# The SwiGLU's last 1024 hidden features: 768 of them by seven products, and a third weight sum made by an adding DMA

## The chip, the cores and the metric

The kernel runs on one core of a Trainium2 chip. The metric is the time of one execution on the device in microseconds (us), lower is better. A core has five engines with queues of their own: PE (matrix products), DVE (vector), ACT (activation), POOL (a second, slower vector engine) and SP (which here only issues DMAs). They meet through semaphores.

## What is computed

One inference step of a hybrid layer over 576 tokens (512 of a prompt, 64 of a sample), 1024 features wide: half a SwiGLU, a mixer, half a SwiGLU, a last norm.

```python
def swiglu(x, w_in, w_out):                  # w_in 1024 x 8192, w_out 4096 x 1024
    a, b = jnp.split(x @ w_in, 2, axis=-1)
    return (jax.nn.silu(a) * b) @ w_out
# layer: x + 1/2 swiglu(norm(x)); + mixer(norm(.)); + 1/2 swiglu(norm(.)); then norm
# mixer: one projection w_in (1024 x 9752), three branches, three projections, gates, w_out
```

All is float32. The transposed activations lie as (128 features) x (8 blocks) x (576 tokens).

## The kernel before

**Products in three parts.** A float32 operand is split into a rounded high part and the rest (`split`: a copy on ACT, L288, a subtraction on DVE, L289). A product is high x high + high x low + low x high, so each 128 x 128 weight block meets each token tile in three matmuls. `ph` and `pl` are the two parts of 512 columns of weights; they live in rings of six.

**Units of seven products.** Most of the work is done in units in the manner of Strassen and Winograd. A unit is two output blocks of 128 features, a reduction over 8 blocks (2 x 4), and two halves of 288 tokens; eight block products become seven. The products are called X1, X2, X3, X4, A11, A22, A21. Each multiplies a weight operand (a block of 128 x 512, or a sum of such blocks) with an activation operand (`T`, for the layer's input, or `T2`, for the hidden features of the SwiGLU). Each is 12 matmuls of 288 columns: 4 blocks x 3 parts (`product`, L616). Results add up in banks of the accumulator: X1, X3, A22, X2 in one, X4 and A21 in a second, A11 in a third, and between two products to one bank ACT or DVE must have read it.

**Weight sums.** For unit n, SP loads two blocks (`fetch_sums`, L460, 512 KB) into `wx`; POOL issues an adding DMA of another 512 KB onto them (L461): X1's operand and X2's. SP loads single blocks into `wr` (L467). In the SwiGLU X3's and X4's operands are made by POOL, in place on X1's tile: add block 2, and later block 3 (L472). In the mixer they go to tiles of their own (`wy`). `stream` works through the units: the operands of a product are made five products ahead (`AHEAD`), and products of two neighbouring units are interleaved by a written-out `order`, where (1, t) is the product t of the unit before:

```python
order = ((0, self.T_X1), (1, self.T_A22), (0, self.T_A11), (1, self.T_A21), (0, self.T_X3), (1, self.T_X2),
         (0, self.T_X4))
```

A planner then sets the order of instructions on every engine, by its own costs and the priorities that the program gives (`high_priority` for reading banks and for the norms).

**A SwiGLU** (`ffn`). The 4096 hidden features are four groups c of 1024, eight units j each. The first four of group 0 are computed plainly (`gemm`, L260), while the operands `T` are made; the rest are units of the stream. When two hidden blocks are ready, `hidden_operands` makes their share of `T2` (five differences on DVE, seven splits), in steps put between products (`tick`). Four units `out(c, m)` then multiply group c with w_out and add to the residual (`residual`, L655); they run between units 1 and 2 of group c + 1. Group 3 is different: its hidden blocks are only split (`hidden_parts`) into YH, YL, which take the place of T2's tiles, and after the stream a plain tail multiplies them with w_out: two passes (i = 6, 7) of 512 rows, eight outputs, two halves of 256 and 320 tokens (`HALVES`). The second pass does most outputs half by half (`half_major`), so that the norm behind it can begin on a finished half while the other is multiplied.

**What follows.** After the first SwiGLU the norm makes XH, XL (`scaled`, L338 and L339), squares (L296, L299, L300) and `rs`, the factor of each token; six plain projections in `branches`, the operands `T` of the mixer (`operands`, L434 to L446), and then the mixer's stream (`pairs`) with 35 units, while the branches' own work runs as jobs between products. After the second SwiGLU `norm_out` squares and scales the output (L299, L396), multiplies the upper half by `rs` (L422) and transposes the lower one (L408 to L415).

The functions that the change touches:

Of the kernel before, what the change touches and what calls it, by code (L numbers as in the profile page):

```python
# [35 lines left out]
NB = 63  # L36
NS = 115
FH = 288
NPLAIN = 4
BUFS = {"g": 9, "t": 5, "P": 4, "Q": 2, "bias": 2}  # L40
# [1 line left out]
FBUFS = {"P": 5, "g": 5, "s": 3}  # L42
# [39 lines left out]
class Hybrid:  # L82
# [112 lines left out]
    def squares(self, tag):  # L195

        pool, bufs = self.sqp
        if pool is self.op:
            return self.op.tile([128, T], F32, name=bufs[tag], tag=bufs[tag], bufs=2)[:, :320]
        return pool.tile([128, 320], F32, name=tag, tag=tag, bufs=bufs[tag])  # L200

    def sm(self):
# [40 lines left out]
        return pool.tile(list(shape), dt, name=tag, tag=tag, bufs=WBUFS[tag])  # L243

    def parts(self, src):
        return self.split(src, self.ring("ph", F32R), self.ring("pl", F32R))

    def col(self, name, n0):

# [202 lines left out]
    def fetch_sums(self, desc):  # L452


        nc = self.nc
        i = len(self.splan)
        self.splan.append(desc)
        src = self.I["sblk"][i].rearrange("p (q c) -> p q c", q=4)
        x12 = self.ring("wx", shape=(128, 2, 512))
        nc.sync.dma_start(x12, src[:, 0:2, :])  # L460
        return {"x12": x12, "src": src}, lambda: nc.gpsimd.dma_start(x12, src[:, 1:3, :], accum_op=ALU.add)  # L461

    def fetch(self, raw):

        for q in (2, 3, 0) if self.mixer else (0, 2, 3):
            raw[q] = self.ring("wr")
            self.nc.sync.dma_start(raw[q], raw["src"][:, q, :])  # L467

    def operand(self, raw, t):

        x12 = raw["x12"]
        add = lambda o, one, two: self.nc.gpsimd.tensor_tensor(o, one, two, op=ALU.add)  # L472
        if not self.mixer:

            if t in (self.T_X3, self.T_X4):
                add(x12[:, 0, :], x12[:, 0, :], raw[2 if t == self.T_X3 else 3])
            x3 = x4 = x12[:, 0, :]
        else:
            if t in (self.T_X3, self.T_X4) and "x3" not in raw:
                raw["x3"], raw["x4"] = self.ring("wy"), self.ring("wy")  # L480
                add(raw["x3"], x12[:, 0, :], raw[2])
                add(raw["x4"], raw["x3"], raw[3])
            x3, x4 = raw.get("x3"), raw.get("x4")
        return self.parts({self.T_X1: x12[:, 0, :], self.T_X2: x12[:, 1, :], self.T_X3: x3, self.T_X4: x4,
                           self.T_A11: raw[0], self.T_A22: raw[2], self.T_A21: raw[3]}[t])

    def stream(self, seq, order, banks):

# [31 lines left out]
    def pairs(self, seq):  # L520

        nc = self.nc
        order = ((0, self.T_X1), (0, self.T_A11), (1, self.T_A22), (0, self.T_X4), (0, self.T_X3), (1, self.T_X2),
                 (0, self.T_A21))
        H = (slice(0, FH), slice(FH, T))

        def tmp(ps, scale):  # L530
            o = self.gp.tile([128, FH], F32, name="uv", tag="uv", bufs=4)
            with self.tc.high_priority(offset=EVAC):
                nc.scalar.activation(o, ps, AF.Copy, scale=scale)  # L533
            return o

        def emit(ps, scale, other=None, op=None):
            def go(dst, a=0, b=FH, func=None):
                with self.tc.high_priority(offset=EVAC):
                    if other is None:
                        nc.scalar.activation(dst, ps[:, a:b], func or AF.Copy, scale=scale)  # L540
                        return
                    nc.vector.scalar_tensor_tensor(dst, ps[:, a:b], scale, other[:, a:b], op0=ALU.mult, op1=op)
                if func:
                    nc.scalar.activation(dst, dst, func)
            return go

        def pair(tiles, done):
            ((name, c1), s1, put1), ((_, c2), s2, put2) = tiles
            o = {}

            def on(t, ps):
                if t == self.T_X1:
                    o["v"] = tmp(ps, s1)
                elif t == self.T_X4:
                    o["m6"] = tmp(ps, s2)
                elif t == self.T_A11:
                    put1(1, H[1], emit(ps, s1, o["v"], ALU.add))
                elif t == self.T_X3:
                    o["u"] = tmp(ps, s2)
                elif t == self.T_A21:  # L560
                    put2(1, H[1], emit(ps, s2, o["u"], ALU.subtract))
                elif t == self.T_A22:
                    put2(0, H[0], emit(ps, -s2, o["m6"], ALU.add))
                else:
                    put1(0, H[0], emit(ps, s1))
                    if done:
                        done()
            return (name, 0, c1, c2), self.T, on
# [40 lines left out]
    def product(self, ps, ops, moving, start):  # L609
        self.tick()  # L610
        hi, lo = ops
        th, tl = moving
        for kk in range(4):
            wsl = slice(kk * 128, (kk + 1) * 128)
            for i, (wt, xx) in enumerate(((hi, th), (hi, tl), (lo, th))):
                self.nc.tensor.matmul(ps, wt[:, wsl], xx[:, kk, :], start=(start and kk == 0 and i == 0),  # L616
                                      stop=(kk == 3 and i == 2), skip_group_check=True)

    def swiglu(self, done):

# [56 lines left out]
            put(one, t)  # L677
            yield 1

    def hidden_parts(self, slot, g):  # L680
        self.split(g.rearrange("p h t -> p (h t)"), self.YH[:, slot, :], self.YL[:, slot, :])
        yield 1

    def ffn(self, x, g0, win, wout, name, last=(0, 1)):

        nc = self.nc
# [21 lines left out]
        def evac_o(ot):  # L710
            def go(h, ps, sl):
                nc.vector.scalar_tensor_tensor(x[:, ot, sl], ps, 0.5, x[:, ot, sl], op0=ALU.mult, op1=ALU.add)
            return go


        def at(c, j):
            return (8 * c + (j if c == 3 else j % 2 * 4 + j // 2)) * 128

        boxes = [{} for _ in range(NPLAIN)]
        tiles = []  # L720
# [17 lines left out]
        got, free = {}, [True]  # L738

        def flush():  # L740

            if not free[0]:
                return
            for c, j in sorted(got):
                if c == 3:
                    self.jobs.append(self.hidden_parts(j, got.pop((c, j))))
                elif j % 2 == 0 and (c, j + 1) in got:
                    self.jobs.append(self.hidden_operands(j // 2, got.pop((c, j)), got.pop((c, j + 1))))
                    if j == 6:
                        free[0] = False  # L750

        def unit(c, j):
            def done(g):
                got[c, j] = g
                flush()
            return (win, 0, 4096 + at(c, j), at(c, j)), self.T, self.swiglu(done)

        def out(c, m):
            def done():
                free[0] = True  # L760
                if c == 2:
                    self.hidden_tiles(name)
                flush()
            return (wout, 1024 * c, 256 * m, 256 * m + 128), self.T2, self.residual(x, m, done if m == 3 else None)

        for j, box in enumerate(boxes):
            got[0, j] = box["g"]
# [765 lines left out]
def pack(plans, inp):  # L1533
    plan, splan = plans
    a = {k: np.asarray(v) for k, v in inp.items()}
    f32 = np.float32
# [15 lines left out]
    sb = np.empty((NS, 128, 4, 4, 128), f32)  # L1552
    for i, (n, r0, c1, c2) in enumerate(splan):
        for q, (c, r) in enumerate(((c1, r0), (c1, r0 + 512), (c2, r0 + 512), (c2, r0))):
            sb[i, :, q] = w[n][r:r + 512, c:c + 128].reshape(4, 128, 128).transpose(1, 0, 2)
# [53 lines left out]
```

## Time and profile before

| | |
|---|---|
| median of three runs | 1939.52 us (1937.3 to 1940.52) |
| the profiled execution | 1944.79 us, its span 1943.1 us |
| granted clock of PE in it | 0.991 |
| units of seven products | 40 + 35 + 40 = 115 |
| the first SwiGLU's stream, by its products | 65.8 to about 532 us |
| the mixer's stream | 626.1 to about 1203 us |
| the second SwiGLU's stream | 1425 to about 1881 us |

Rows of the profile name the source line of the kernel before (L616), the engine, the tiles written and read (out<-in, buffer numbers left out), a count, and then busy time, mean duration of one in ns, and the idle time of the engine just before, with what ended it. PE is a matmul, PEld the load of its weights. Matmuls are pipelined: one takes 0.3 us by its record, while the next starts 0.12 to 0.15 us after it. A stretch's row has the busy us and the number of instructions of PE, PEld, DVE, ACT and POOL, the granted clock, the share of the DMA engines, and GB/s. A row of waits has the total, the number and the longest.

### The profile page before, as it was taken

How to read it: one execution, taken by the hardware profiler on the slowest of the kernel's cores; microseconds unless marked ns; L12 is line 12 of the kernel's file. 1: busy time of each engine (PE TensorE's matmuls, PEld its weight loads, DVE VectorE, ACT ScalarE, POOL GpSimd, SP SyncE). 2: the span in 40 equal slices, each digit the busy share in tenths (PEclk: the TensorE clock that was granted, in tenths of full speed). 3: DMA queues.
4: the chain of work that ended last, by engine and by line, in shares of the span. 5: the costliest groups of instructions: out<-in, count | busy, mean ns of one | idle time of the engine just before them, and what ended most of it. 6: DMA issues, size and time to landing. Idle time of an engine off the chain costs nothing. (4 is left out here: it accounts for less than half of the span.)

```text
span 1943.1 us, 37678 instructions
## 1 busy us (share of the span) xinstructions
PE 1887.2 (97%) x13901; PEld 1823.6 (94%) x13901; DVE 1524.6 (78%) x2715; ACT 1089.5 (56%) x2486; POOL 680.1 (35%) x656
## 2 busy tenths in 40 slices
PE   9999999999999999999999998999999999999998
PEld 8899999999999878888888888999999999999998
DVE  8998998988768767667777775745898888988865
ACT  4554654655544777767675765324555455554544
POOL 5343333333202234323435353440233334334311
PEclk9999999999999999899999999999999999999999
DMA  7267666666742545753667557742236666666631
GB/s 241 74 160 173 159 163 163 159 172 163 185 131 80 156 117 159 200 147 108 183 165 183 155 152 213 241 143 88 77 99 165 163 157 172 166 157 167 159 94 60
DMA packets 129440, 294.69 MB, mean 152 GB/s; under 512 B 14289, under 2 KB 26193, under 8 KB 129257
## 3 DMA queue, kind: packets, MB, share of 16 engines
q1 hardware_dynamic: 100072, 205.67, 32.7%
q0 software_dynamic: 19696, 72.10, 20.5%
q10 hardware_dynamic: 9488, 14.53, 2.6%
q8 instruction: 109, 1.79, 0.4%
q14 instruction: 75, 0.61, 0.1%
HBM read 272.87 MB, written 19.38 MB: 150 GB/s over the span
## 5 line engine op out<-in xcount | busy, mean ns | idle before, releaser
L616 PE MATMUL acc<-TH,ph 128*128 128x288 f32 x3220 | 968.0, 301 | 27.4 <-ACT uv L533 11.8
L616 PE MATMUL acc<-TL,ph 128*128 128x288 f32 x3220 | 955.4, 297 | 0.6 <-DVE TL L289 0.6
L616 PE MATMUL acc<-TH,pl 128*128 128x288 f32 x3220 | 955.0, 298 | 1.0 <-DVE pl L289 0.9
L616 PEld LDWEIGHTS acc<-TH,ph 128*128 128x128 f32 x3220 | 607.5, 189 | 46.9 <-ACT uv L533 15.5
L616 PEld LDWEIGHTS acc<-TL,ph 128*128 128x128 f32 x3220 | 609.4, 189 | 4.9 <-issue 3.7
L616 PEld LDWEIGHTS acc<-TH,pl 128*128 128x128 f32 x3220 | 608.4, 189 | 4.8 <-DVE pl L289 2.2
L289 DVE TENSOR_TENSOR pl<-wr,ph 128x512 fp32r<-128x512 f32 x471 | 429.4, 919 | 76.9 <-ACT ph L288 64.5
L288 ACT CAST ph<-wr 128x512 fp32r<-128x512 f32 x471 | 287.9, 620 | 267.9 <-PE acc L616 141.3
L289 DVE TENSOR_TENSOR pl<-wx,ph 128x512 fp32r<-128x512 f32 x390 | 328.1, 845 | 44.5 <-ACT ph L288 37.9
L288 ACT CAST ph<-wx 128x512 fp32r<-128x512 f32 x390 | 237.4, 621 | 201.3 <-POOL wx L472 110.2
L472 POOL TENSOR_TENSOR wx<-wx,wr 128x512 f32<-128x512 f32 x160 | 246.3, 1539 | 188.2 <-DVE pl L289 150.4
L461 POOL DMA_DIRECT2D wx<-in_sblk x115 | 101.6, 901 | 524.1 <-DMA wx<-in_sblk 154.7
L260 PE MATMUL acc<-YH,ph 128*128 128x256 f32 (+1 forms) x768 | 226.5, 298 | 6.3 <-ACT YH L288 5.8
L260 PE MATMUL acc<-YL,ph 128*128 128x320 f32 (+1 forms) x768 | 227.1, 297 | 2.3 <-DVE YL L339 1.9
L260 PE MATMUL acc<-YH,pl 128*128 128x256 f32 (+1 forms) x768 | 226.5, 296 | 0.1
L260 PEld LDWEIGHTS acc<-YH,ph 128*128 128x128 f32 x768 | 145.4, 190 | 6.9 <-ACT YH L288 5.9
L260 PEld LDWEIGHTS acc<-YL,ph 128*128 128x128 f32 x768 | 145.4, 189 | 3.5 <-DVE YL L339 3.3
L260 PEld LDWEIGHTS acc<-YH,pl 128*128 128x128 f32 x768 | 145.2, 189 | 0.3 <-DVE pl L289 0.3
L472 POOL TENSOR_TENSOR wy<-wx,wr 128x512 f32<-128x512 f32 x35 | 56.2, 1605 | 136.0 <-DVE pl L289 120.0
L655 DVE SCALAR_TENSOR_TENSOR R<-acc,R 128x288 f32<-128x288 f32 x168 | 75.7, 450 | 18.6 <-PE acc L616 18.1
L288 ACT CAST TH<-g 128x288 fp32r<-128x288 f32 x120 | 51.6, 434 | 59.8 <-POOL g L641 34.6
L289 DVE TENSOR_TENSOR pl<-wy,ph 128x512 fp32r<-128x512 f32 x70 | 59.8, 857 | 29.6 <-ACT ph L288 26.6
(320 smaller groups left out, 2393.4 us busy)
## 6 DMA issues: line engine op xcount, KB each, us to landing
wr<-in_sblk SPq DMA_DIRECT2D x345, 256.0 KB, 3.6
wx<-in_sblk SPq DMA_DIRECT2D x115, 512.0 KB, 3.8
wx<-in_sblk POOLq DMA_DIRECT2D x115, 512.0 KB, 6.8
wr<-in_wblk SPq DMA_DIRECT2D x126, 256.0 KB, 3.0
R<-scr_rows ACTq DMA_DIRECT2D x12, 576.0 KB, 5.9
gs<-g SPq DMA_DIRECT2D x20, 288.0 KB, 4.5
g<-gs POOLq DMA_DIRECT2D x20, 288.0 KB, 3.9
y<-ys POOLq DMA_DIRECT2D x12, 288.0 KB, 3.8
```

The source lines that it names most:

```text
L260: nc.tensor.matmul(ps[:, :n], wt[:, wsl], xx[:, k0 + k, a:a + n], start=(k == 0 and i == 0), stop=(k == nk - 1 and i == 2))
L288: self.nc.scalar.copy(hi, src)
L289: self.nc.vector.tensor_tensor(lo, src, hi.bitcast(F32), op=ALU.subtract)
L461: return {"x12": x12, "src": src}, lambda: nc.gpsimd.dma_start(x12, src[:, 1:3, :], accum_op=ALU.add)
L472: add = lambda o, one, two: self.nc.gpsimd.tensor_tensor(o, one, two, op=ALU.add)
L616: self.nc.tensor.matmul(ps, wt[:, wsl], xx[:, kk, :], start=(start and kk == 0 and i == 0), stop=(kk == 3 and i == 2), skip_group_check=True)
L655: self.nc.vector.scalar_tensor_tensor(o, ps, scale, o, op0=ALU.mult, op1=ALU.add)
```

## The change

1. Group 3: six of its eight hidden blocks go through `hidden_operands` like the others, and four units `out(3, m)` with three row blocks in place of four end the stream (a product of theirs has 9 matmuls). The last two hidden blocks are split into the fourth slots of T2's tiles X1, A11, X4, A22 (`rest`), and a plain tail of 256 rows multiplies them, both halves of outputs 0 to 5, then 6 and 7 half by half, in halves of 288 tokens. T2 stays; YH and YL don't come back.
2. In all units the third sum (X3) is made by an adding DMA of block 2 onto X1's operand, issued by POOL when X1 has been split. POOL adds block 3 for X4. In the SwiGLU's order X2 of the unit before now precedes X3; in the mixer's X3 precedes X4.
3. The squares of the last norm take tiles of the rings `wr` and `g`.

```diff
     def operand(self, raw, t):
-        x12 = raw["x12"]
-        add = lambda o, one, two: self.nc.gpsimd.tensor_tensor(o, one, two, op=ALU.add)
-        if not self.mixer:
-            if t in (self.T_X3, self.T_X4):
-                add(x12[:, 0, :], x12[:, 0, :], raw[2 if t == self.T_X3 else 3])
-            x3 = x4 = x12[:, 0, :]
-        else:
...
+        nc, x12 = self.nc, raw["x12"]
+        x4 = x13 = x12[:, 0, :]
+        if t == self.T_X4:
+            if self.mixer:
+                x4 = self.ring("wy")
+            nc.gpsimd.tensor_tensor(x4, x13, raw[3], op=ALU.add)
+        parts = self.parts({self.T_X1: x13, self.T_X2: x12[:, 1, :], self.T_X3: x13, self.T_X4: x4,
+                            self.T_A11: raw[0], self.T_A22: raw[2], self.T_A21: raw[3]}[t])
+        if t == self.T_X1:
+            nc.gpsimd.dma_start(x13, raw["src"][:, 2, :], accum_op=ALU.add)
+        return parts
...
-        order = ((0, self.T_X1), (0, self.T_A11), (1, self.T_A22), (0, self.T_X4), (0, self.T_X3), (1, self.T_X2),
+        order = ((0, self.T_X1), (0, self.T_A11), (1, self.T_A22), (0, self.T_X3), (0, self.T_X4), (1, self.T_X2),
                  (0, self.T_A21))
...
-        for kk in range(4):
+        nk = hi.shape[1] // 128
+        for kk in range(nk):
...
-    def hidden_parts(self, slot, g):
-        self.split(g.rearrange("p h t -> p (h t)"), self.YH[:, slot, :], self.YL[:, slot, :])
-        yield 1
+    def rest(self, k, h):
+        return [v[:, 3, :] for v in self.T2[(self.T_X1, self.T_A11, self.T_X4, self.T_A22)[2 * k + h]]]
+    def hidden_parts(self, k, g):
+        for h in range(2):
+            self.split(g[:, h, :], *self.rest(k, h))
+            yield 1
...
-                if c == 2:
-                    self.hidden_tiles(name)
...
+        seq += [out(3, m) for m in range(4)]
-        order = ((0, self.T_X1), (1, self.T_A22), (0, self.T_A11), (1, self.T_A21), (0, self.T_X3), (1, self.T_X2),
+        order = ((0, self.T_X1), (1, self.T_A22), (0, self.T_A11), (1, self.T_A21), (1, self.T_X2), (0, self.T_X3),
                  (0, self.T_X4))
         self.stream(seq, order, lambda n: {self.T_X1: n % 3, self.T_A11: 3, self.T_X4: 4 + n % 2})
         self.drain()
-        for i in (6, 7):
-            tiles = [((wout, i * 512, 512, j * 256, 256), [(0, evac_o(2 * j)), (128, evac_o(2 * j + 1))])
-                     for j in range(4)]
-            n = 1 if i == 7 else 4
-            self.gemm(tiles[:n], self.YH, self.YL, k0=(i % 2) * 4)
-            self.gemm(tiles[n:], self.YH, self.YL, k0=(i % 2) * 4, half_major=True, order=last)
+        wt = {}
+        for n, halves in [(n, (0, 1)) for n in range(6)] + [(n, (h,)) for h in last for n in (6, 7)]:
+            m = n // 4
+            if m not in wt:
+                wt[m] = self.weights((wout, 3840, 256, m * 512, 512))
+            for h in halves:
+                ps = self.bank()[:, :FH]
+                for k, (hi, lo) in enumerate(wt[m]):
+                    th, tl = self.rest(k, h)
+                    wsl = slice(n % 4 * 128, n % 4 * 128 + 128)
+                    for i, (w, t) in enumerate(((hi, th), (hi, tl), (lo, th))):
+                        nc.tensor.matmul(ps, w[:, wsl], t, start=(k == 0 and i == 0), stop=(k == 1 and i == 2))
+                evac_o(n)(h, ps, slice(h * FH, (h + 1) * FH))
+        self.sqp = self.wp, None
```

More of the change, by code (lines that the diff above doesn't have):

```diff
@@ L35 @@
 CH = [(0, 128), (128, 128), (256, 128), (384, 128), (512, 64)]
-NB = 63
-NS = 115
+NB = 51
+NS = 123
 FH = 288
@@ L199, in squares @@
             return self.op.tile([128, T], F32, name=bufs[tag], tag=bufs[tag], bufs=2)[:, :320]
+        if pool is self.wp:
+            o = self.ring("wr") if tag == "na" else pool.tile([128, T], F32, name="g", tag="g", bufs=FBUFS["g"])
+            return o[:, :320]
         return pool.tile([128, 320], F32, name=tag, tag=tag, bufs=bufs[tag])
@@ L245, in parts @@
     def parts(self, src):
-        return self.split(src, self.ring("ph", F32R), self.ring("pl", F32R))
+        n = src.shape[1]
+        return self.split(src, self.ring("ph", F32R)[:, :n], self.ring("pl", F32R)[:, :n])
     def col(self, name, n0):
@@ L465, in fetch @@
         for q in (2, 3, 0) if self.mixer else (0, 2, 3):
-            raw[q] = self.ring("wr")
+            raw[q] = self.ring("wr")[:, :raw["src"].shape[2]]
             self.nc.sync.dma_start(raw[q], raw["src"][:, q, :])
     def operand(self, raw, t):
-        x12 = raw["x12"]
-        add = lambda o, one, two: self.nc.gpsimd.tensor_tensor(o, one, two, op=ALU.add)
-        if not self.mixer:
-            if t in (self.T_X3, self.T_X4):
-                add(x12[:, 0, :], x12[:, 0, :], raw[2 if t == self.T_X3 else 3])
-            x3 = x4 = x12[:, 0, :]
-        else:
[L479 to L485, printed above, removed]
+        nc, x12 = self.nc, raw["x12"]
[9 more added lines that the diff above has]
+        return parts
     def stream(self, seq, order, banks):
@@ L567, in on @@
                         done()
-            return (name, 0, c1, c2), self.T, on
+            return (name, 0, c1, c2, 4), self.T, on
         self.stream([pair(*p) for p in seq], order, lambda n: {self.T_X1: n % 2, self.T_X4: 2, self.T_A11: 2})
@@ L616, in product @@
                 self.nc.tensor.matmul(ps, wt[:, wsl], xx[:, kk, :], start=(start and kk == 0 and i == 0),
-                                      stop=(kk == 3 and i == 2), skip_group_check=True)
+                                      stop=(kk == nk - 1 and i == 2), skip_group_check=True)
     def swiglu(self, done):
@@ L716, in at @@
         def at(c, j):
-            return (8 * c + (j if c == 3 else j % 2 * 4 + j // 2)) * 128
+            return (8 * c + (j if c == 3 and j > 5 else j % 2 * (3 if c == 3 else 4) + j // 2)) * 128
         boxes = [{} for _ in range(NPLAIN)]
@@ L744, in flush @@
             for c, j in sorted(got):
-                if c == 3:
-                    self.jobs.append(self.hidden_parts(j, got.pop((c, j))))
+                if c == 3 and j > 5:
+                    self.jobs.append(self.hidden_parts(j - 6, got.pop((c, j))))
                 elif j % 2 == 0 and (c, j + 1) in got:
@@ L755, in done @@
                 flush()
-            return (win, 0, 4096 + at(c, j), at(c, j)), self.T, self.swiglu(done)
+            return (win, 0, 4096 + at(c, j), at(c, j), 4), self.T, self.swiglu(done)
         def out(c, m):
@@ L760, in done @@
                 free[0] = True
[L761 to L762 removed]
                 flush()
[L764 removed]
+            return ((wout, 1024 * c, 256 * m, 256 * m + 128, 3 if c == 3 else 4), self.T2,
+                    self.residual(x, m, done if m == 3 else None))
         for j, box in enumerate(boxes):
@@ L1550, in pack @@
     out["wblk"] = wb
[L1552 to L1555, printed above, removed]
+    sb = np.zeros((NS, 128, 4, 4, 128), f32)
+    for i, (n, r0, c1, c2, nk) in enumerate(splan):
+        r1 = r0 + nk * 128
+        for q, (c, r) in enumerate(((c1, r0), (c1, r1), (c2, r1), (c2, r0))):
+            sb[i, :, q, :nk] = w[n][r:r + nk * 128, c:c + 128].reshape(nk, 128, 128).transpose(1, 0, 2)
     out["sblk"] = sb.reshape(NS, 128, 2048)
```

5 lines of the change are left out of this document (3 added, 2 removed).

## The prediction

> **What bounds the kernel now.** I read the page's first part, then the chain that ended last, then the waits of PE by stretch, then busy time by stretch.
>
> ```profile
> span 1943.1 us, 37678 instructions
> PE 1887.2 (97%) x13901; PEld 1823.6 (94%) x13901; DVE 1524.6 (78%) x2715; ACT 1089.5 (56%) x2486; POOL 680.1 (35%) x656
> ...
> 1763.66 110.58 PE acc L616 x828
> ...
> 1926.14 3.48 PE acc L260 x28
> ...
> 1930.47 0.44 ACT rs L401
> ...
> 1930.97 4.39 POOL R L422 x4
> ```
>
> PE is busy 97% of the span and the chain is PE work up to its last 13 us, so time falls only when matmuls go or PE's waits shrink. A matmul of the seven-product stream costs 110.58/828 = 0.1336 us on the chain. The two tails hold the plain matmuls that the change attacks, and the end hangs on the last norm (rs, then four multiplies, then the output). Waits of PE, in the first SwiGLU's stream (60 to 90 and 90 to 520), the mixer (626 to 1203) and the second stream (1330 to 1870):
>
> ```profile
> PE acc L616 <- ACT TH L288: 1.7, 2, 1.0
> ...
> PE acc L616 <- ACT g L627: 1.3, 3, 0.6
> PE acc L616 <- DVE P L635: 0.8, 3, 0.3
> ...
> PE acc L616 <- ACT uv L533: 11.8, 12, 2.9
> PE acc L616 <- DVE g L542: 4.6, 4, 1.6
> ...
> PE acc L616 <- DVE P L635: 1.2, 5, 0.3
> PE acc L616 <- ACT g L627: 1.1, 3, 0.5
> ```
>
> The streams wait little: about 5 us in the first (3.1 of it at 60 to 90) and 2.7 in the second. Busy time by stretch (PE, PEld, DVE, ACT, POOL): late units of a block, the last block, the plain tail, the mixer's opening, the second tail.
>
> ```profile
> 204.00:272.00 68.00, 67.67 (x506) 67.21 (x505) 64.49 (x102) 41.53 (x92) 25.48 (x23) 1.00 0.60 159
> 452.00:520.00 68.00, 68.00 (x512) 68.00 (x512) 56.64 (x75) 39.03 (x76) 24.59 (x22) 1.00 0.66 168
> 534.00:576.00 42.00, 42.00 (x318) 42.00 (x318) 25.71 (x53) 15.68 (x29) 0.24 (x1) 1.00 0.41 127
> 577.00:625.00 48.00, 46.11 (x346) 45.63 (x344) 41.62 (x79) 23.82 (x47) 11.25 (x10) 1.00 0.28 93
> ```
>
> DVE is the second bound: 64.49 of 68 us in a block, where it falls behind PE.
>
> **The change, part by part.**
>
> *1. Fewer matmuls.* Per SwiGLU the plain tail has 8 row blocks x 8 outputs x 2 halves x 3 = 384 matmuls, 768 in both. After: 4 units x 7 products x 3 blocks x 3 = 252, and 2 blocks x 8 x 2 x 3 = 96, so 348. Plain ones cost 42.00/318 = 0.1321 us (they alternate 256 and 320 columns), the new ones, all of 288, 0.1336: 768 x 0.1321 - 696 x 0.1336 = 101.5 - 93.0 = **-8.5 us**. All lies on PE's path.
>
> *2. The third sum.* In the streams X3's add on POOL goes, and a 256 KB adding DMA comes, issued by POOL once X1 is split; X4's add stays.
>
> ```profile
> L472 POOL TENSOR_TENSOR wx<-wx,wr 128x512 f32<-128x512 f32 x160 | 246.3, 1539 | 188.2 <-DVE pl L289 150.4 <-issue 34.5 <-ACT TH L288 3.3
> ...
> L461 POOL DMA_DIRECT2D wx<-in_sblk x115: 837/881/1902, 26.9 to 1835.9; - x115
> DMA to landing us min/median/max: 5.4/6.8/15.8
> ...
> 247.71 1.60 POOL L472 TENSOR_TENSOR wx<-wx,wr 128x512 f32<-128x512 f32 x1
> 248.99 1.08 POOL L641 TENSOR_TENSOR g<-g,P 128x288 f32<-128x288 f32 x1
> ...
> 248.16 3.08 DVE L289 TENSOR_TENSOR pl<-wr,ph 128x512 fp32r<-128x512 f32 x2
> ...
> 255.39 0.69 DVE L289 TENSOR_TENSOR pl<-wx,ph 128x512 fp32r<-128x512 f32 x1
> ...
> g<-gs POOLq DMA_DIRECT2D x20, 288.0 KB, 3.9
> ```
>
> POOL's time itself costs nothing (25 of 68 us busy). But two splits beside POOL's add and multiply took 3.08 us, not 2 x 0.69: 1.7 us more for 1.9 us of overlap, 0.89 per us. An add of 1.54 us thus costs DVE up to 1.4 us of a unit's 11 (none if DVE is then at work from PSUM); I take 1.0. That ends DVE's falling behind. What it can return to PE is bounded by the streams' waits, about 8 us; against it, the new order leaves two products, not three, between A22 and X2 (3.2 us, not 4.8) in which DVE must read the bank, and X4 comes right behind X3. I take **-2 us** (-7 to +6).
>
> Does the sum come in time? X3's split stands five products behind X1's, some 8 us. A DMA of 256 KB lies between the plain 288 KB (3.9 us to landing) and the adding 512 KB (6.8); I take 5, midway. With X1's split (0.62 + 0.69) and POOL's turn it lands 6.5 to 7.5 us after X1's split began: just hidden, with the splits' own lead (some 4 us before use) behind it. Without that cover each us late costs each of the 88 stream units up to 1 us. POOL's queue now waits for X1's split before the next unit's 512 KB DMA and X4's add; both have room. The Trainium skill, DMA: Bandwidth & Descriptors, section Anatomy of one DMA, fits a GpSimd DMA as 2.0 us plus bytes at 436 GB/s: an estimate of 2.6 us for this one and 3.2 for 512 KB. The 6.8 measured for the latter speaks against it here. By that rule rival B would have next to no chance, and the sum would stay.
>
> *3. The mixer.* 35 units get the same DMA (their wy adds halve too), and X3 ahead of X4: A11's bank has one product more before X4 needs it, X4's has one fewer before A21. Its 24 us of waits (first rows above) come from ACT and DVE reading banks late. X3 stands only three products behind X1, but a unit there takes (1203 - 626)/35 = 16 us, so a product's step is 2.3 us. DVE gains up to 1 us a unit; ACT can be held by an X3 split whose sum hasn't landed, with the bank reads queued behind it. **-0.5 us** (-6 to +10).
>
> *4. The last blocks* get three more sets of hidden operands in place of plain splits.
>
> ```profile
> L289 DVE TENSOR_TENSOR TL<-g,TH 128x288 fp32r<-128x288 f32 x120 | 56.7, 475 | 17.2 <-ACT TH L288 17.2
> ...
> L664 DVE TENSOR_TENSOR P<-g 128x288 f32<-128x288 f32 x48 | 40.3, 877 | 0.0
> L664 DVE TENSOR_TENSOR g<-g 128x288 f32<-128x288 f32 x72 | 35.1, 488 | 0.1
> ```
>
> A set is 2 x 0.88 + 3 x 0.49 + 7 x 0.48 = 6.6 us of DVE, less the two whole-width splits it replaces (twice a half-width one each, 1.9): 4.7; three sets are 14 of the 68 us, against 11 idle there and 6 freed by part 2. Products of 9 matmuls leave bank reads two products or 2.4 us: **+0.5** (0 to +3).
>
> *5. From the first SwiGLU to the mixer.* This is where cover goes.
>
> ```profile
> 560.48 0.48 DVE L339 SCALAR_TENSOR_TENSOR XL<-R,cst,XH 128x256 fp32r<-128x256 f32 x1 [0.19 <-ACT XH L338]
> ...
> 576.25 0.41 ACT L296 ACTIVATE xd<-R 128x256 f32<-128x256 f32 x1
> ...
> 578.34 0.55 DVE L339 SCALAR_TENSOR_TENSOR XL<-R,cst,XH 128x320 fp32r<-128x320 f32 x1
> 578.80 5.43 DVE L300 TENSOR_TENSOR xd<-xd,xk 128x256 f32<-128x256 f32 x10
> ...
> 593.55 0.43 ACT L354 COPY rs<-ps_x 128x320 f32<-128x320 f32 x1 [1.79 <-PE ps_x L330]
> ...
> 625.48 0.30 PE L794 MATMUL ps_x<-ident,R 24*128 24x24 f32 x2 [2.37 <-DVE R L1488]
> ```
>
> Before, 15 of the 16 XL pieces were made under the plain tail. Now T2 lives to the tail's last product, and in the program XH and XL lie partly on its bytes (XH's 18432 bytes begin at 147520, T2's first tile, X1, at 164832; XL ends at 184384, inside A11's), as xd lay partly on YH's and had to wait until 576.25. X1 is read to the last product of half 0, A11 to the last of half 1. So XH can start only 1.6 us before the tail's end, XL only behind it: 8 x (0.48 + 0.55) = 8.2 us of DVE work moves behind the tail, in front of rs. PE meets the first XL about 1 us late and then eats them nearly as fast as DVE makes them, helped by having two or three tiles to turn to. DVE, busy 41.62 of the 48 us to the mixer's first product, and made up at 625.48 with a wait of 2.37 us already, takes the rest: 8.2 less some 2 us of idle it can use, less the two adds that leave this stretch (2 to 3 us). **+3 us** (0 to +8).
>
> *6. The end.* The second tail lasts 96 x 0.1336 = 12.8 us, and every output is final only there; the norm's upper half starts at column 256, so it needs both half products of an output.
>
> ```profile
> 1920.25 0.47 ACT L299 ACTIVATE sq<-R 128x320 f32<-128x320 f32 x1 [0.69 <-DVE R L712]
> 1920.75 0.57 ACT L396 ACTIVATE R<-R,cst 128x320 f32<-128x320 f32 x1
> 1923.55 0.40 ACT L299 ACTIVATE sq<-R 128x256 f32<-128x256 f32 x1
> ...
> 1930.79 0.51 ACT L396 ACTIVATE R<-R,cst 128x256 f32<-128x256 f32 x1
> ...
> 1934.56 0.41 DVE L712 SCALAR_TENSOR_TENSOR R<-acc,R 128x256 f32<-128x256 f32 x1
> ```
>
> ACT has 8 x (0.47 + 0.57 + 0.40 + 0.51) = 15.6 us there and gets its first piece 1.6 us in: it ends about 5 us after PE, and rs comes about 5.4 us after PE's last product. Before, PE's last plain product was at 1929.6 by the chain, rs at 1930.9 and the span's end at 1943.1: 12.2 us behind rs, much of it the L422 multiplies and the last output, whose evacuation (1934.56) was itself late. If both paths run as before from rs on: 5.4 + 12.2 = 17.6 us; if the output path, free of that late evacuation, goes ahead: about 14.4. Before it was 13.5. **+2 us** (0 to +4).
>
> *Sum:* -8.5 - 2 - 0.5 + 0.5 + 3 + 2 = **-5.5 us**. The profiled execution took 1944.79 us (span 1943.1); it stands 5.3 us over the median of 1939.52, so it would be 1939.3, and the median 1934.0. About 0.2% (3.9 us) is what can be told from no change here.
>
> **Rivals.** *B, slower: the third sum is late.* Place: ACT's queue at X3's split, in the mixer above all. For it: the adding 512 KB has taken up to 15.8 us, and DMA engines at 0.60 to 0.66 busy get some 31 MB more (123 times 256 KB). It decides where landing passes about 9 us or POOL issues late: if 35 mixer units wait 0.5 us each, +17, so 1951. Against it: the median of 6.8 us for twice the bytes. The skill's SBUF page (SBUF — State Buffer, SBUF: two separate sides) has a rule for such a delay: a GpSimd DMA cannot write its descriptors while DVE holds the port they share. The issue's 837/881 ns minimum and median, with DVE busy 95% of a stretch, shows none of it. I leave it 0.03 of B's chance.
> *C: the ends are covered.* The planner fits the norms in, and waits of the streams vanish: -8.5 - 5 + 1 = -12.5, so 1927. For it: DVE idle in the tail (25.71 of 42).
> *D: the ends eat it.* Parts 5 and 6 at their upper bounds, +12, the rest as above: +1.5, so 1941; with one of them only, 1937.
>
> **How the numbers follow.** Forecast (1929 to 1939) 0.45, B 0.15, C 0.2, D 0.2. Faster by over 0.2% (under 1935.6): C and three quarters of the forecast, 0.54; within: the rest of the forecast and D, 0.31; slower: B, 0.15. Range 1925 to 1945: it leaves out most of B and C's far edge.
>
> **What would show it.** Right: the stream's three forms up by 168 each, the plain YH forms down by 256 each and a new line with 64 each; POOL's adds on wx halved; DVE's splits (0.69 alone) shorter on average and DVE under 60 of 68 us in the late units of a block; PE waits under 5 us in both streams; a PE wait on XL at the mixer's start; rs later behind PE at the end. Wrong: PE waits on ACT ph or pl in the streams, mixer waits far over 24 us, or no shift in the tails.

## The result, and the profile after

The changed kernel takes 2070.45 us (median of four runs, 2064.73 to 2078.09) beside 1939.72 us for the kernel before on the same chip: 1.0673 times as long (95% interval 1.0644 to 1.0703), 131 us slower. The forecast was 1934.0 and the range ended at 1945.

The page of the changed kernel: the span, busy time by engine, then groups of instructions (busy us, mean ns | idle time of the engine just before, and what ended most of it), then two rows of its list of DMAs (KB, median us from issue to landing).

```profile
span 2064.8 us, 37841 instructions
...
PE 1927.4 (93%) x13829; PEld 1845.0 (89%) x13829; DVE 1387.9 (67%) x2835; ACT 1083.1 (52%) x2552; POOL 636.4 (31%) x680
...
L620 PE MATMUL acc<-TH,ph 128*128 128x288 f32 x3388 | 1028.4, 305 | 77.0 <-DVE P L639 22.6
...
L293 ACT CAST ph<-wx 128x512 fp32r<-128x512 f32 (+1 forms) x457 | 271.3, 611 | 519.7 <-DMA wx<-in_sblk 325.6
L294 DVE TENSOR_TENSOR pl<-wr,ph 128x512 fp32r<-128x512 f32 (+1 forms) x471 | 334.8, 714 | 43.3 <-ACT ph L293 38.7
...
L483 POOL TENSOR_TENSOR wx<-wx,wr 128x512 f32<-128x512 f32 (+1 forms) x88 | 128.2, 1457 | 490.4 <-DVE pl L294 490.4
...
wx<-in_sblk POOLq DMA_DIRECT2D x115, 512.0 KB, 5.6
wx<-in_sblk POOLq DMA_DIRECT2D x115, 256.0 KB, 6.0
```

DVE has lost 137 us of work and PE has 72 matmuls fewer, as the change intends. Yet PE is busy for 40 us longer, and idle for 81 us more. The row to stop at is ACT's: before its splits of wx, ACT stood 325.6 us for the DMA. In the kernel before, the waits listed for ACT in its three streams name no such DMA; the largest two of its first stream are shown below. By stretch, between the first and the last product of each stream as they stand in the two traces (in the kernel before, the first stream's last product is at 526.7 and the mixer's at 1209.2): the first SwiGLU's stream with the way to the mixer took 560.3 us and takes 582.6; the mixer's stream 582.8 and 655.8; the projections behind the mixer 216.3 both times; the second SwiGLU's stream with the end 517.9 and 544.1. So of 121.7 us of span 22 are in the first SwiGLU, 73 in the mixer and 26 in the second SwiGLU.

Waits of ACT in the kernel before, in the first stream (65 to 526), then in the changed kernel, in the first stream (66 to 588), the mixer (648 to 1304) and the second stream (1520 to 2035): us in total, how often, the longest.

```profile
ACT ph L288 <- PE acc L616: 70.5, 85, 2.6
ACT ph L288 <- POOL wx L472: 60.0, 44, 3.4
...
ACT ph L293 <- DMA wx<-in_sblk: 101.7, 34, 6.5
ACT ph L293 <- POOL wx L483: 56.2, 32, 3.6
...
ACT ph L293 <- DMA wx<-in_sblk: 107.6, 27, 8.7
...
ACT ph L293 <- DMA wx<-in_sblk: 111.3, 34, 7.0
```

One unit of the first stream in the changed kernel, in the order of time within each engine (start, us, what, in brackets the idle time before it and what ended it): ACT, DVE, POOL, PE. Two rows of the mixer follow.

```profile
249.64 1.14 ACT L293 CAST ph<-wx 128x512 fp32r<-128x512 f32 x2
...
255.50 0.39 ACT L636 COPY P<-acc 128x288 f32<-128x288 f32 x1
258.98 0.62 ACT L293 CAST ph<-wx 128x512 fp32r<-128x512 f32 x1 [3.09 <-DMA wx<-in_sblk]
259.51 0.39 ACT L636 COPY P<-acc 128x288 f32<-128x288 f32 x1
...
261.72 1.14 ACT L293 CAST ph<-wx 128x512 fp32r<-128x512 f32 x2 [1.52 <-POOL wx L483]
...
251.63 0.68 DVE L294 TENSOR_TENSOR pl<-wx,ph 128x512 fp32r<-128x512 f32 x1
...
262.37 0.69 DVE L294 TENSOR_TENSOR pl<-wx,ph 128x512 fp32r<-128x512 f32 x1 [2.05 <-ACT ph L293]
262.98 0.45 DVE L639 TENSOR_TENSOR P<-P,acc 128x288 f32<-128x288 f32 x1
...
250.53 0.87 POOL L468 DMA_DIRECT2D wx<-in_sblk  x1 [1.59 <-DMA wx<-in_sblk]
252.61 0.86 POOL L487 DMA_DIRECT2D wx<-in_sblk  x1 [1.20 <-DVE pl L294]
...
260.40 1.28 POOL L483 TENSOR_TENSOR wx<-wx,wr 128x512 f32<-128x512 f32 x1 [5.38 <-DVE pl L294]
...
263.48 0.40 PE L620 MATMUL acc<-TH,ph 128*128 128x288 f32 x1 [0.60 <-DVE P L639]
...
1023.00 0.62 ACT L293 CAST ph<-wx 128x512 fp32r<-128x512 f32 x1 [4.19 <-DMA wx<-in_sblk]
...
1024.41 0.39 ACT L536 ACTIVATE uv<-acc 128x288 f32<-128x288 f32 x1
...
1024.86 0.47 PE L620 MATMUL acc<-TH,ph 128*128 128x288 f32 x1 [2.29 <-ACT uv L536]
```

Read it from X1. ACT splits X1 in the pair at 249.64, DVE's half of the split ends at 252.3, and POOL issues the sum's DMA (L487) at 252.61, 2.1 us behind a 512 KB adding DMA (L468). It lands 6.4 us later, at 258.98. But ACT had come to X3's split at 255.9, and ACT takes its instructions in order: the bank read at 259.51 and X4's sum (L483 at 260.40) and split (in the pair at 261.72) stand behind it. DVE runs dry (2.05 us), the bank is read late (262.98), and PE waits for that read. In the mixer it takes fewer steps: the bank read `uv` stands in ACT's queue behind a split that waited 4.19 us, and PE stands 2.29 us. PE's own waits name DVE P, ACT uv or ACT P, hardly ever the DMA; only the waits of the engine in between show the cause.

Busy time by stretch (PE, PEld, DVE, ACT, POOL, then granted clock, share of the DMA engines, GB/s): the mixer's stream before, then after.

```profile
626.00:1209.00 583.00, 557.04 (x4025) 504.08 (x4023) 411.74 (x873) 406.02 (x1105) 224.17 (x231) 0.98 0.59 158
```

```profile
648.00:1304.00 656.00, 586.23 (x4024) 526.51 (x4025) 399.25 (x884) 405.37 (x1110) 204.10 (x233) 0.93 0.61 154
```

The same matmuls keep PE busy 29 us longer, at a granted clock of 0.93 in place of 0.98. So the mixer's 73 us are about 44 us of waiting and 29 us of slower matmuls. The changed kernel's whole trace has 23 stretches of low clock where that of the kernel before has 7; all of them are at 0.50.

### The profile page after: what moved, and what is told of

It reads as the page before. It is cut to its first block, busy times and chain, and to the rows that moved or that the text cites. A ratio compares the mean times of both kernels' runs of the same rounds, so it can differ in the third digit from the quotient of the medians.

```text
span 2064.8 us, 37841 instructions
## 1 busy us (share of the span) xinstructions
PE 1927.4 (93%) x13829; PEld 1845.0 (89%) x13829; DVE 1387.9 (67%) x2835; ACT 1083.1 (52%) x2552; POOL 636.4 (31%) x680
## 5 line engine op out<-in xcount | busy, mean ns | idle before, releaser
L620 PE MATMUL acc<-TH,ph 128*128 128x288 f32 x3388 | 1028.4, 305 | 77.0 <-DVE P L639 22.6
L294 DVE TENSOR_TENSOR pl<-wx,ph 128x512 fp32r<-128x512 f32 (+1 forms) x457 | 325.0, 716 | 401.2 <-ACT ph L293 393.5
L293 ACT CAST ph<-wx 128x512 fp32r<-128x512 f32 (+1 forms) x457 | 271.3, 611 | 519.7 <-DMA wx<-in_sblk 325.6
L294 DVE TENSOR_TENSOR pl<-wr,ph 128x512 fp32r<-128x512 f32 (+1 forms) x471 | 334.8, 714 | 43.3 <-ACT ph L293 38.7
L293 ACT CAST ph<-wr 128x512 fp32r<-128x512 f32 (+1 forms) x471 | 278.3, 609 | 127.2 <-PE acc L265 61.8
L483 POOL TENSOR_TENSOR wx<-wx,wr 128x512 f32<-128x512 f32 (+1 forms) x88 | 128.2, 1457 | 490.4 <-DVE pl L294 490.4
L468 POOL DMA_DIRECT2D wx<-in_sblk x123 | 111.9, 926 | 235.2 <-DMA wx<-in_sblk 123.9
L487 POOL DMA_DIRECT2D wx<-in_sblk x123 | 113.5, 923 | 198.1 <-DVE pl L294 179.0
L265 PE MATMUL acc<-YH,ph 128*128 128x320 f32 (+1 forms) x512 | 152.2, 300 | 5.4 <-ACT YH L293 5.1
L265 PE MATMUL acc<-YL,ph 128*128 128x256 f32 (+1 forms) x512 | 152.6, 300 | 3.0 <-DVE YL L344 2.5
L265 PE MATMUL acc<-YH,pl 128*128 128x320 f32 (+1 forms) x512 | 151.4, 297 | 0.0
L483 POOL TENSOR_TENSOR wy<-wx,wr 128x512 f32<-128x512 f32 x35 | 47.0, 1343 | 156.3 <-DMA wx<-in_sblk 138.3
```

The lines of the kernel that those rows point to most:

```text
L265: nc.tensor.matmul(ps[:, :n], wt[:, wsl], xx[:, k0 + k, a:a + n], start=(k == 0 and i == 0), stop=(k == nk - 1 and i == 2))
L293: self.nc.scalar.copy(hi, src)
L294: self.nc.vector.tensor_tensor(lo, src, hi.bitcast(F32), op=ALU.subtract)
L483: nc.gpsimd.tensor_tensor(x4, x13, raw[3], op=ALU.add)
L487: nc.gpsimd.dma_start(x13, raw["src"][:, 2, :], accum_op=ALU.add)
```

## The experiments

Four theories were set against each other. L: the sum comes too late for X3's place in ACT's queue. M: the bytes load the DMA engines. O: the new orders starve the banks. E: the new last blocks and tails cost the time. Q came in later: POOL's own queue, where an instruction that waits holds up the sums and DMAs behind it.

**tail_only**: the changed kernel with part 2 taken back.

```diff
-            nc.gpsimd.dma_start(x13, raw["src"][:, 2, :], accum_op=ALU.add)
+            # operand() and both orders as before: POOL adds raw[2], then raw[3]
```

> The change with its part 2 left out: the new tails (part 1) as they are, but the third sum added by POOL from raw[2] as before, and both old orders of products. Theory L (the late sum: X3's split stands in ACT's queue before its DMA has landed, DVE and the bank reads stand behind it): no wait of that kind is left, so what remains is the tails' own sum of the prediction, -8.5 + 0.5 + 3 + 2 = -3, about 1937 (1930 to 1945). Theory M (memory load: 31 MB more on the DMA engines slow every load): the same, since the 31 MB go too. Theory O (the new orders of products starve the banks): the same. Theory E (the new last blocks and tails cost the time): most of the 131 us stays, over 2030.

Measured: 1940.58 us, 1.0024 times before (1.0011 to 1.0036). E falls. But the tails don't pay either: a little slower where -3 us was expected.

**sum_only**: the kernel before with part 2 alone (`operand` and the two orders of the change).

> The kernel before with part 2 alone: the adding DMA makes the third sum in all 115 units, with the two new orders, and the old plain tails. L and M: nearly the whole loss, 1939.7 + 131 + 3 = about 2074 (2055 to 2085; 8 units fewer than in the changed kernel would take off some 5). O: the same, as the orders are in it. E: 1940.

Measured: 2037.6 us, 1.0519 (1.0501 to 1.0537). Part 2 alone costs some 100 us, less than any theory but E had it: the two SwiGLU streams are 20 and 14 us longer than before, the mixer 60 (642.4 for 582.8). Beside the new tails the loss grows by another 33 us, of which the spans show 19 in the two SwiGLUs, with four units more each, and 13 in the mixer. Why the mixer, which is the same in both, loses more there was not followed up.

**orders_only**: the kernel before with the two new orders alone.

> The kernel before with the two new orders of products alone (SwiGLU: X2 of the unit before ahead of X3; mixer: X3 ahead of X4), POOL adding all sums. L and M: no late sum and no more traffic, 1940 within 5. O: the two streams grow by some 26 each and the mixer by 73, about 2065.

Measured: 1931.15 us, 0.9969 (0.9955 to 0.9982). O falls with the opposite sign: the orders gain some 6 us, most of it in the mixer (576.1 for 582.8) and the second stream (452.2 for 455.5). One more run, orders_tail, has the new tails and the new orders, with POOL adding all sums. If the two effects simply added, 0.9993 was expected; it took 1934.84 us, 0.998 (0.9968 to 0.9993).

**mixer_pool**: the changed kernel, with the mixer's sums and order as before.

```diff
+        if self.mixer:
+            if t in (self.T_X3, self.T_X4) and "x3" not in raw:
+                raw["x3"], raw["x4"] = self.ring("wy"), self.ring("wy")
+                add(raw["x3"], x12[:, 0, :], raw[2])
+                add(raw["x4"], raw["x3"], raw[3])
...
-        if t == self.T_X1:
+        if t == self.T_X1 and not self.mixer:
```

> The changed kernel with the mixer's part put back: in its 35 units POOL adds the third sum and the old order stands; both SwiGLUs keep the adding DMA. L: the mixer's stream returns from 656 to about 583 us, the SwiGLU streams stay at 522 and 515, so 2070.5 - 73 = about 1997. M: the mixer carries 9 MB less of the 31; the SwiGLU streams, in other stretches, don't notice; the same 1997. O: the same. E: the mixer stays near 656, about 2065.

Measured: 1989.78 us, 1.0269 (1.0248 to 1.029). The mixer is back at 579.9 us. The time that it loses by the lower clock (the length of each stretch times the share not granted) is 10 us, as in the kernel before, where it was 43 in the changed one. The SwiGLU streams stay at 525 and 510. The three stretches pay each for itself.

**lead_swiglu** (on mixer_pool) and **lead_all** (on the changed kernel): more time between X1's split and X3's, in the SwiGLUs or everywhere.

```diff
+        for n, t in uses:
+            if (n, t) in skip: continue
+            if t == self.T_X3 and n + 1 < len(seq):      # lead_swiglu: and not self.mixer
+                skip.add((n + 1, self.T_X1))
+                makes += [(n, t), (n + 1, self.T_X1)] if self.mixer else [(n + 1, self.T_X1), (n, t)]
+            else: makes.append((n, t))
...
-            for u in uses[(i + AHEAD if i else 0):i + AHEAD + 1]:
+            for u in makes[(i + AHEAD if i else 0):i + AHEAD + 1]:
...
+            with self.tc.issue_after(self.cut) if t == self.T_X3 else nullcontext():   # cut: ACT's last split
                 ops[n, t] = self.operand(raw[n], t)
```

> mixer_pool (1989.8) with the DMA kept in the SwiGLUs, but more time for it: X1 of the next unit is split before X3 of this one, two operands earlier than in the change, and X3's split is queued on ACT behind it, so some 8 products lie between the two splits in place of 4 to 5. Same bytes, same POOL issues, same wait of POOL for X1's split. Theory L (ACT stands at X3's split because its DMA lands too late): the waits on the DMA, 102 and 111 us of ACT in the two streams of the changed kernel, go, and the streams return from 525 and 510 to tail_only's 498 and 489: 1990 - 48 = about 1942 (1935 to 1950). Theory M (memory load): no change, 1990. Theory Q (POOL's queue: its wait for X1's split holds up X4's add and the next 512 KB DMA): no change, 1990, as POOL waits for the same thing.

> The changed kernel (2070.5) with the same lead in the SwiGLUs, and in the mixer X1 of the next unit split right behind X3 of this one, so six operands in place of three lie between X1's split and X3's. L: the SwiGLUs give back 48; in the mixer three products more are some 7 us at its pace of 16 us a unit, more than the 2.7 us that ACT stood at a late X3, so its stream returns from 656 to about 585: 2070.5 - 48 - 70 = about 1952 (1940 to 1975). M and Q: no change, 2070.

Measured: lead_swiglu 2020.08 us, 1.0415 (1.0388 to 1.0443), 30 us slower than mixer_pool where 48 us faster was expected; lead_all 2006.65 us, 1.0359 (1.0336 to 1.0382). In lead_all the mixer takes 571.8 us: there L is confirmed, and M can't explain it, since the bytes are the same. In the SwiGLUs the expectation missed. Waits of lead_all in its first stream (ACT, then POOL), and a unit of lead_swiglu (POOL, then ACT):

```profile
ACT ph L293 <- POOL wx L483: 174.7, 41, 8.4
...
POOL wx L468 <- DMA wx<-in_sblk: 130.5, 43, 5.6
```

```profile
253.98 0.86 POOL L468 DMA_DIRECT2D wx<-in_sblk  x1 [3.62 <-DMA wx<-in_sblk]
254.54 1.62 POOL L479 TENSOR_TENSOR wx<-wx,wr 128x512 f32<-128x512 f32 x1
...
256.20 0.62 ACT L293 CAST ph<-wx 128x512 fp32r<-128x512 f32 x1 [3.73 <-POOL wx L479]
```

ACT's wait for the DMA is gone, and a wait for X4's add has taken its place. The earlier X1 had also drawn the 512 KB DMA of a later unit ahead (L468): its issue stands on POOL for SyncE's load of the tile, and X4's add stands behind it.

**lead_begin_all**: lead_all with that DMA queued behind X4's add in the SwiGLUs. It is called the mended change below. **sum_lead_begin**: the same on the kernel before, with its old tails.

```diff
-                if m in begin and (m < n + 2 or t == self.T_X3):
+                if m in begin and (m < 2 if not self.mixer else m < n + 2 or t == self.T_X3):
                     begin.pop(m)()
...
+            if not self.mixer and t == self.T_X4 and n + 2 in begin:
+                with self.tc.issue_after(self.x4add):
+                    begin.pop(n + 2)()
```

> lead_all (2006.7, SwiGLU streams 534 and 525, mixer 572) with one thing moved on POOL's queue in the SwiGLUs: the 512 KB adding DMA for unit n + 2 is queued behind X4's add of unit n, in place of ahead of it. In lead_all that DMA's issue stood 118 us (38 times) in the first stream for SyncE's plain load of the same tile, with X4's add behind it, for which ACT waited 164 us. Theory Q (what is left in the SwiGLUs is X4's add standing in POOL's queue): the streams return to those of orders_tail, 494 and 485, and with the mixer at 572 the total is 2006.7 - 40 - 40 = about 1927 (1920 to 1940). Theory M (the memory load): some 31 us stay, as in load_only: about 1958. Theory L without Q (only ACT's place of X3's split mattered, and that is mended already): no change, 2007.

> The same two moves on the kernel before, with its old tails: so sum_only (2037.6) with X1 split earlier, X3's split queued behind it, and the 512 KB DMA behind X4's add. Q: orders_only's time (1931), less some 4 us that the mixer showed in lead_all (572 against 576), less what is left of the streams' waits, so 1922 to 1931: faster than the kernel before. M: 31 us more, about 1960. L without Q: about 2037 - 84 + 80, 2035.

Measured: lead_begin_all 1925.09 us, 0.992 (0.9905 to 0.9936); sum_lead_begin 1921.44 us, 0.9906 (0.9889 to 0.9923). Both are faster than the kernel before and than the change. The mended change has every byte, every operation and every tail of the change; only the places of some instructions in the queues differ. Beside the kernels with the same orders and tails whose sums POOL adds (orders_tail 0.998, orders_only 0.9969), the adding DMA gains 0.6% in both, some 12 us. Of lead_begin_all: ACT's waits in the first stream, the issues of POOL in one unit of it, and busy time in the mixer, the second stream, and late units of a block.

```profile
ACT ph L293 <- PE acc L634: 100.2, 129, 1.8
ACT ph L293 <- POOL wx L483: 44.4, 28, 2.7
...
ACT ph L293 <- DMA wx<-in_sblk: 9.3, 8, 2.0
...
250.16 0.87 POOL L487 DMA_DIRECT2D wx<-in_sblk  x1 [3.87 <-DVE pl L294]
251.50 1.28 POOL L483 TENSOR_TENSOR wx<-wx,wr 128x512 f32<-128x512 f32 x1 [0.47 <-DVE pl L294]
252.74 0.85 POOL L468 DMA_DIRECT2D wx<-in_sblk  x1
...
618.00:1191.00 573.00, 551.02 (x4016) 499.51 (x4015) 399.20 (x882) 404.99 (x1109) 199.93 (x229) 0.99 0.68 176
1410.00:1893.00 483.00, 483.00 (x3632) 483.00 (x3631) 369.71 (x715) 267.10 (x556) 157.01 (x154) 1.00 0.74 179
...
204.00:272.00 68.00, 68.00 (x514) 68.00 (x513) 51.88 (x102) 43.26 (x94) 25.47 (x24) 1.00 0.77 189
```

ACT now waits mostly for PE to free its buffers, which means that it is ahead; in the second stream PE is busy throughout. In the SwiGLUs the sum's DMA is now issued ahead of the 512 KB one, and the sum lands 6.1 to 6.6 us after X1's split began (medians of the two streams and the mixer). How much of the gain is this earlier landing and how much X3's later place was not separated. The DMA engines are busier than in the changed kernel (0.68 in the mixer against 0.61), which speaks against M.

**load_only**, **load_nowait**, **load_sp**: orders_only with 256 KB more a unit that nobody reads.

```diff
+        if t == self.T_X1:
+            extra = self.nc.gpsimd.dma_start(self.spare, raw["src"][:, 2, :], accum_op=ALU.add).ins
+            # load_only: extra waits for X1's split; load_nowait: same place, no wait
+            # load_sp: self.nc.sync.dma_start(spare[i % 4], ...), a plain copy, no wait
```

> orders_only (1931.2, the sums all added by POOL) with one more 256 KB adding DMA in each of the 115 units, of the same source rows, issued by POOL where the change issues it and waiting for X1's split like it, but onto a DRAM tile that nobody reads: there was no room for it in SBUF. L: the load itself costs little, 1931 to 1940. M: the streams grow by 20 to 25 each and the mixer by some 60, 2030 or more. Q: as M, 2030, since POOL's queue has the same waits.

> load_only (1970.2) with one wait taken away: the spare adding DMA stands at the same place of POOL's queue, but doesn't wait for X1's split (the two tiles have nothing in common, so nothing is at risk). The bytes are the same. Q: the +39 us come from POOL standing there with the sums of X3 and X4 behind it, so nearly all goes: 1931 to 1942. M: they come from the bytes or from the issue itself, so nothing goes: 1970.

> load_nowait (1971.5: orders_only with a spare 256 KB adding DMA a unit, issued by POOL, waiting for nothing of X1) with the spare transfer issued by SyncE as a plain copy of the same source rows to four DRAM tiles in turn that nobody reads. Theory M (the bytes cost the 39 us): about 1970 again. Theory P (POOL's own time for one more issue a unit, 0.87 us in front of the sums, or the software queue behind it): back to orders_only, 1931 to 1938, unless SyncE's loads now stand behind the copy.

Measured: 1970.22 us, 1.0167 (1.0154 to 1.0181); 1971.54 us, 1.0166 (1.0142 to 1.019); 1934.93 us, 0.9953 (0.9934 to 0.9972), beside orders_only's 0.9969. The two DMA rows of load_nowait and load_sp, each with its median us to landing:

```profile
spare<-in_sblk POOLq DMA_DIRECT2D x115, 256.0 KB, 7.6
```

```profile
spare<-in_sblk SPq DMA_DIRECT2D x115, 256.0 KB, 4.9
```

None of the three expectations for load_only had it right (1931 to 1940, or 2030). The same bytes from SyncE's queue cost nothing that can be told: M falls. The wait for X1's split isn't it either, against what Q expected: 39 us come with one more adding DMA a unit on POOL, waiting or not. Whether that is POOL's time in front of its two sums or the adding into DRAM was not separated. In the mended change POOL issues as many DMAs, but adds one sum a unit instead of two, and nothing is lost.

## Why the prediction was wrong, step by step

**Part 2, "Does the sum come in time?", is the step that failed.** It set a sum 6.5 to 7.5 us after X1's split began against 8 us, "X3's split stands five products behind X1's". The first number was 0.4 to 1.4 us too small in the two streams. Over the 34 splits of X3 that waited in each of them, in the median: from the start of X1's split to the end of DVE's half 1.78 us (1.31 assumed), from issue to landing 5.9 to 6.0 (5 assumed), in all 7.9. The traces show with what the landing goes: 82 of the 86 DMAs for a sum in the two streams were issued while a 512 KB adding DMA of the same queue was still under way, which the forecast didn't count; in the mended change 1 of 84 was, and they took 4.4 to 4.5 us. The second number was the larger error in the streams. Five products is the distance of the products on PE; in ACT's queue the planner had put X3's split earlier, and ACT reached it 5.2 to 5.7 us after it began X1's. The lead of the splits before their use, which was counted as further cover, protects PE from a late split. It doesn't protect what stands behind the split in the same queue.

**The mixer (part 3) was the same wait with a larger price**: -0.5 us forecast, 73 measured. Here the landing was the larger error. At the 27 splits that waited, ACT came 7.7 us after it began X1's, near the three products of 2.3 us that were counted, but the sum landed only after 11.3 (medians). From issue to landing it took 8.1 us in the median where a 512 KB adding DMA was still under way (20 units) and 4.9 where none was (14). The mechanism was named there ("ACT can be held by an X3 split whose sum hasn't landed, with the bank reads queued behind it") and is rival B's, place and all. B's price was wrong: 0.5 us for each of 35 mixer units, 17 in all, where ACT waited 107.6 us in the mixer, 3.1 us a unit, and lost 2.1 us of time a unit; and the streams, where ACT stood 102 and 111 us, gave another 48, 0.55 us for each of their 88 units. Its chance of 0.15 rested on the two numbers above.

**A term was missing: the clock.** 29 us of the mixer's 73 are matmuls at a lower clock. A wait of PE in the mixer thus costs more than its length, and the loss goes when the waits go (lead_begin_all, 0.99). The Trainium skill, TensorE: Matmul & The Clock Gate, Part 1, says that the clock falls to half after an idle window of about 3.4 us. The traces agree in kind: every low stretch is granted 0.50 and most last 3.41 us or a small multiple of it.

**The new DMA's own time.** From issue to landing it took 6.0 us in the median, and its issue lasts 0.87 us, like that of the old one (0.88). The fit of the Trainium skill, DMA: Bandwidth & Descriptors, Anatomy of one DMA, gave the prediction an estimate of 2.6 us for it; the measurement speaks against it, and B would have been dismissed by it. The rule of the shared port in the Trainium skill, SBUF — State Buffer, SBUF: two separate sides, by which DVE's work can hold up such a DMA, still shows nothing in the length of the issue.

**Right: what part 2 frees.** DVE's work beside POOL's adds was indeed lengthened by them. Splits of `wr` fell from 919 to 714 ns, where the new orders alone leave them at 923. DVE's busy time in the late units of a block fell from 64.49 us of 68 to 51.88 in the mended change. But 5.7 us of this come with the orders alone:

```profile
204.00:272.00 68.00, 68.00 (x514) 68.00 (x513) 58.77 (x101) 41.77 (x93) 29.52 (x24) 1.00 0.60 160
```

So the sum's share is 6.9 us, 1.15 for each of the six units there, close to the 1.0 taken. The orders were the wrong part: the forecast counted them against the gain, and they help. With the waits mended, PE's pauses over 0.135 us a matmul, summed over a stream from the trace, fall from 11.4 and 6.2 us to 8.3 and 0.4, which is 9 us, where 2 were taken; the orders alone bring them to 9.9 and 2.1. In the mixer the orders alone gain 7 us, and with the sum by DMA (sum_lead_begin) it is 15, where 0.5 was forecast.

**Part 1 right in its counts**: 168 more of each stream form, 512 YH matmuls where there were 768, 64 of each in the new tail. **Parts 4 to 6** can be read in tail_only, where nothing hides them. Part 4: the first stream grew by 37.3 us where its 252 new matmuls take 33.7, so +3.6; the second by 33.6, so nothing; forecast +0.5, up to 3. Part 5: the way to the mixer shrank by 35.9 us, 2.0 less than the matmuls taken away; forecast +3, and as forecast PE waits there, but only 1.1 us for XH and 0.4 for XL (PE's waits in tail_only between the stream and the mixer):

```profile
PE acc L265 <- ACT XH L343: 1.1, 1, 1.1
...
PE acc L265 <- DVE XL L344: 0.4, 1, 0.4
```

Part 6: the last tail product, and `rs`, of the kernel before and then of tail_only:

```profile
1931.41 0.28 PE L260 MATMUL acc<-YH,pl 128*128 128x256 f32 x1
...
1930.47 0.43 ACT L401 COPY rs<-ps_x 128x320 f32<-128x320 f32 x1 [0.25 <-PE ps_x L330]
```

```profile
1922.92 0.29 PE L801 MATMUL acc<-TH,pl 128*128 128x288 f32 x1
...
1929.27 0.41 ACT L406 COPY rs<-ps_x 128x320 f32<-128x320 f32 x1
```

From `rs` to the end it is 12.0 us in tail_only against 12.2 forecast, and `rs` comes 6.3 us behind the last product, against 5.4. But the kernel before had `rs` 0.9 us ahead of its last product: the chain's link that ended at 1929.6 was taken for the last plain matmul, which starts at 1931.41. From last product to end it was 11.7 us, not 13.5, and is 18.3. So the end costs 6.6 us by this measure, and 4.8 by the span behind the stream's last product, which shrank by 33.1 us for 37.9 us of matmuls; not 2. Together parts 4 to 6 cost more (some 10 us) than the 8.5 us of matmuls saved: rival D is what the tails do by themselves, and with the queues mended the old tails are as good as the new ones (0.9906 and 0.992, intervals that overlap).

## What to carry to other kernels

When a step goes from an engine to a DMA, set its landing against the place of the first consumer in that engine's instruction queue, and look at what stands behind it and at what its own queue still has under way when it is issued; the distance of the uses on the bound engine is not the cover. A wait that is mended in one queue can come up in another: follow the wait of the engine in between (ACT, then POOL here) until it waits only for the bound engine. A forecast should price such a wait for every unit in which it recurs, and add the clock that PE loses by it.

## What the runs showed of the hardware that was not expected

- The same 256 KB adding DMA took 6.0 us to landing in the median in the changed kernel, 4.8 in lead_all and 4.5 in lead_begin_all, where the DMA engines were busier. It goes with a 512 KB adding DMA of the same queue that was still under way at its issue (in the changed kernel's mixer 8.1 us with one, 4.9 without), and not with the load, which was higher where it was shorter; no run changed this alone.
- One more adding DMA a unit on POOL's queue, into DRAM, cost 39 us with or without its wait, and the same bytes from SyncE nothing.
- The longest wait listed for PE in the mixer was 5.4 us, and yet PE's busy time for the same matmuls rose by 29 us, at a granted clock of 0.93 in place of 0.98.
